# An encoder layer on one core: the first two feed-forward tiles without Strassen, the down GEMM's first sums on VectorE, one norm's sums two tiles later

## The chip, the cores and the metric

The kernel runs on one NeuronCore of a Trainium2 chip. The metric is the device time of one execution in microseconds; lower is better. Three executions of the kernel before took 1586.12, 1586.13 and 1588.37 us, the median is 1586.13 us. The engines are named as the profile names them: PE is the matrix engine (TensorE), DVE is VectorE, ACT is ScalarE, POOL is GpSimd, and SP is the engine whose queue issues nearly all DMAs.

## The reference

One layer of a streaming encoder is computed for 1024 prompt frames and 8 x 16 sample frames, together 1152 rows of 1024 features. Cut to what matters here:

```python
x  = x + rmsnorm(merged @ w_out, g_post1)          # output GEMM, first residual
h2 = rmsnorm(x, g_pre2)
up = h2 @ w_ffn_up                                 # 1024 -> 2 x 2816
a, g = split(up)
act = gelu(causal_conv3(a) + b_dw) * g
x  = x + rmsnorm(act @ w_ffn_down, g_post2)        # 2816 -> 1024
```

Ahead of it lie the three branches (state space, pooling, memory attention) and their gates, which the change does not touch. Everything is float32. The reference's tolerance is met by splitting each operand into a high and a low part of a reduced 32-bit type, so that one product takes three matmuls: high x high, high x low, low x high.

## The kernel before

**Layout.** Activations lie transposed: 128 features on the partitions, rows along the free axis, in three chunks of 384 rows (chunk 0, 1, 2). A weight tile is 128 output features by eight blocks of 128 inputs. One output tile for one chunk is thus 8 x 3 = 24 matmuls of 128x384 (`proj`, which calls `mm3`), collected in one PSUM bank. There are four banks with the tag `c` (in the profile `pc`) and four with the tag `s` (`ps`).

**Splitting.** `split` makes the high part by an ACT copy and the low part by a DVE subtraction, unless it is given another engine. In the profile these are the pairs `whi`/`wlo` (weights), `mhi`/`mlo`, `h2hi`/`h2lo`, `bB`/`bT` (operands of the up GEMM), `dhi`/`dlo` and `dB` (operands of the down GEMM). Both lines of `split` (L63, L64) serve all of them.

**The output GEMM** (`phase_o`) runs over the chunks and in each over eight tiles f of 128 features (`out`). ACT copies each result out of PSUM into `merged` (in the profile `mg`) and squares it; DVE adds the squares into `ssa`. `sums` brings the sums of squares over the partitions by one-column matmuls on PE (L1072) and takes the inverse root on POOL (L86). `row_bcast` spreads that over the partitions: three ACT operations (`diag`, L94) and one PE matmul (L96). `resid` applies the first norm and adds the input x, which it loads two tiles at a time; it writes the sum back to DRAM (`Dx2`) and collects a second sum of squares. `norm` applies the second norm. The sums, the resid and the norm of chunk c-1 are woven between the tiles of chunk c; for chunk 1 the second `sums` stands behind tile f = 4 of chunk 2 (`NF = (0, 5, 4)`), which is where PE asks for it. Chunk 2 itself has no following chunk: its resid and norm are woven into the first work of the up GEMM.

**The up GEMM** treats 22 tiles ff, each of one tile of `a` and one of `g`. For chunks 0 and 1 it uses Strassen's method in Winograd's form over (a, g) x (two halves of the 1024 inputs): seven products of 12 matmuls instead of eight, thus 84 matmuls for both tiles and both chunks instead of 96. This needs four sums of weights per tile (`up_w`: S1 to S4, each then split) and four sums of activations, made once (T1 to T4, split once; B11, B21, B22 and in the change B12 are the quarters themselves). `up_prod` issues one product and evacuates it. Chunk 2 is always done plainly (`up_last`). For ff = 0 and 1 the weight sums are made on DVE, for later ones on POOL. In `phase_u` the two first tiles load and split their weights a second time for chunk 2, since the Strassen operands took the buffers:

```python
for s in self.first:
    self.raws[s.ff] = self.up_raw(s.ff)
    s.aw = self.load_w(None, pool=self.w2, r=self.raws[s.ff][0])
    self.up_last(s, "a"); self.up_act(s); self.up_wg(s); ...
```

**The down GEMM** (`phase_d`) takes 22 blocks of 128 inputs: two whole ones first (`first`, 24 banks of six matmuls), then four groups of four by the same seven-product method, then four whole ones. Products are added up by DVE in SBUF tiles `M` and `y2` (`evac`, L1476 and L1478; the four subtractions of L1608 belong to the first part). A `group` is a generator that loads, sums and splits the operands of one group while PE works on the part ahead of it; its eight sums (L1436 to L1439 for weights, L1444 to L1447 for activations) and four of its splits (S1 to S4) run on POOL.

**What sets the order.** The program is emitted in the order of the Python code, and a scheduler then orders each engine's queue by a simulated timeline. High priority, `issue_after` and `keep_in_program_order` bend this by hand. Each engine then runs its queue strictly in order, and so does SP with its DMAs.

Of the kernel before, what the change touches and what calls it, by code (L numbers as in the profile page):

```python
# [32 lines left out]
class K:  # L33
# [27 lines left out]
    def split(self, hi, lo, src, eng=None):  # L61
        nc = self.nc
        nc.scalar.activation(hi, src, AF.Copy)  # L63
        (eng or nc.vector).tensor_sub(lo, src, hi)  # L64

    def load_raw(self, src, shape=(128, 8, 128)):
# [963 lines left out]
    def phase_o(self):  # L1030
# [6 lines left out]
        if True:  # L1037
# [75 lines left out]
            def norm(c, rs):  # L1113
# [9 lines left out]
                for f in range(8):  # L1123
                    V.scalar_tensor_tensor(oT[:, f, :], oT[:, f, :], self.vec[:, V_GPRE2 + f:V_GPRE2 + f + 1], rb,  # L1124
                                           op0=OP.mult, op1=OP.mult)
                    if c == 2:
                        self.split(self.hhi2[:, f, :], self.hlo2[f], oT[:, f, :])

# [5 lines left out]
            ss = []  # L1134
            NF = (0, 5, 4)
            self.B = {}
            lo, up = slice(0, 4), slice(4, 8)
            h0, h1 = self.merged[0], self.merged[1]
            for c in range(3):
                ss.append(ssa())  # L1140
                for f in range(8):
                    self.pin_sq = c == 2
                    if c == 2 and f == 2:
                        self.raws = {0: self.up_raw(0)}
                    out(c, f)
                    if c:
# [16 lines left out]
            s0 = self.up_begin(0)  # L1163
            self.up_w(s0)

            op("B22", h1[:, up])
            V.tensor_sub(h0[:, lo], h1[:, lo], h0[:, lo])
            V.tensor_sub(h1[:, lo], h1[:, up], h1[:, lo])
            V.tensor_sub(h1[:, up], h1[:, up], h0[:, lo])
            op("T2", h1[:, up])  # L1170
            op("T1", h0[:, lo])
            V.tensor_sub(h0[:, up], h0[:, up], h1[:, lo])
            op("T3", h1[:, lo])
            op("T4", h0[:, up])
            self.raws[1] = self.up_raw(1)
            s1 = self.up_begin(1)

            def prods(s, *ps):
                for p in ps:
                    self.up_prod(s, p)  # L1180
# [12 lines left out]
            norm(2, rs)  # L1193
            prods(s1, 7, 3, 4)
            self.first = s0, s1

# [24 lines left out]
    def up_w(self, s, eng=(None,) * 4):  # L1221

        G = self.nc.vector if s.ff < 2 else self.nc.gpsimd
        ra, rg = self.raws[s.ff]
# [13 lines left out]
        s1, s2 = stage()  # L1238
# [15 lines left out]
    def up_prod(self, s, p):  # L1254
# [95 lines left out]
    def phase_d(self):  # L1350
# [6 lines left out]
        with ExitStack() as ctx:  # L1357
# [42 lines left out]
            def group(g):  # L1400

                s = _S()
                s.g, s.A, s.B = g, {}, {}
                yield s
# [39 lines left out]
                G.tensor_sub(b11, b12, b11)  # L1444
                G.tensor_sub(b12, b22, b12)
                G.tensor_sub(b22, b22, b11)
                G.tensor_sub(b21, b21, b22)  # L1447
# [396 lines left out]
```

## Time and profile before

| | |
|---|---|
| median of three executions | 1586.13 us |
| the profiled execution: time, span | 1587.11 us, 1585.3 us |
| mean granted PE clock | 0.984 |
| PE busy | 97% of the span |
| DVE, ACT, POOL busy | 65%, 37%, 31% |
| DMA | 163.44 MB, mean 103 GB/s |

The profile is that of one execution, whose time is 1.81 us above its span and 0.98 us above the median of the three. PE is busy nearly all the time, so what matters is where it is not, and where its granted clock falls. The slices of the page show two such places inside the kernel: the clock digits fall to 8 in slices 19 and 20 of 40 (each 39.6 us long), which is the passage from the output GEMM to the up GEMM, and DVE is at 8 and 7 tenths around slice 34, where the down GEMM starts. "Busy" of a matmul overlaps the next one's, so a rate is read from starts, not from durations.

### The profile page before, as it was taken

How to read it: one execution, taken by the hardware profiler on the slowest of the kernel's cores; microseconds unless marked ns; L12 is line 12 of the kernel's file. 1: busy time of each engine (PE TensorE's matmuls, PEld its weight loads, DVE VectorE, ACT ScalarE, POOL GpSimd, SP SyncE). 2: the span in 40 equal slices, each digit the busy share in tenths (PEclk: the TensorE clock that was granted, in tenths of full speed). 3: DMA queues.
4: the chain of work that ended last, by engine and by line, in shares of the span. 5: the costliest groups of instructions: out<-in, count | busy, mean ns of one | idle time of the engine just before them, and what ended most of it. 6: DMA issues, size and time to landing. Idle time of an engine off the chain costs nothing.

```text
span 1585.3 us, 22927 instructions
## 1 busy us (share of the span) xinstructions
PE 1539.2 (97%) x8964; PEld 1506.2 (95%) x8964; DVE 1035.0 (65%) x1619; ACT 589.0 (37%) x902; POOL 487.1 (31%) x447
## 2 busy tenths in 40 slices
PE   7999999999999999998989999999999999999996
PEld 7999998888999999998979999999999998999996
DVE  7956986656533463648777655665656569788866
ACT  8313444434312250534444333333333343233321
POOL 0000010000111234200025444444344327665546
PEclk9999999999999999999889999999999999999998
DMA  7533334422422244223123121212121234122315
GB/s 266 168 102 102 107 108 162 151 88 75 158 75 70 81 128 138 98 92 108 47 100 128 56 84 71 83 55 84 70 70 69 80 128 141 60 100 95 92 64 169
DMA packets 98604, 163.44 MB, mean 103 GB/s; under 512 B 23232, under 2 KB 68672, under 8 KB 98496
## 3 DMA queue, kind: packets, MB, share of 16 engines
q1 hardware_dynamic: 98064, 161.75, 31.0%
q8 instruction: 70, 1.15, 0.3%
q14 instruction: 38, 0.31, 0.1%
q10 hardware_dynamic: 432, 0.23, 0.0%
HBM read 119.52 MB, written 42.42 MB: 102 GB/s over the span
## 4 chain that ended last, share of the span: by engine, by line
PE 81%; DVE 9%; DMA 3%; ACT 3%; issue 2%; POOL 1%; SPq 0%; POOLq 0%; DVEq 0%; ACTq 0%
PE pc L107 15%; PE pc L103 15%; PE pc L106 15%; PE ps L103 11%; PE ps L106 11%; PE ps L107 11%; DVE dB L64 1%; DMA Ts<-DG 1%; PE ps L849 1%; DMA DG<-gs 1%; ACT hhi L126 1%; DMA dwr<-in_w_down 1%; PE ps L1072 1%; DVE mg L1124 1%; DVE wlo L64 0%
## 5 line engine op out<-in xcount | busy, mean ns | idle before, releaser
L103 PE MATMUL pc<-hhi,whi 128*128 128x384 f32 x760 | 258.2, 340 | 6.6 <-ACT hhi L126 6.6
L107 PE MATMUL pc<-hhi,wlo 128*128 128x384 f32 x760 | 257.1, 339 | 0.7 <-DVE wlo L64 0.7
L106 PE MATMUL pc<-hlo,whi 128*128 128x384 f32 x760 | 257.5, 339 | 0.1
L63 ACT ACTIVATE whi<-rawt 128x1024 fp32r<-128x1024 f32 (+1 forms) x103 | 107.7, 1046 | 187.0 <-PE pc L106 86.5
L64 DVE TENSOR_TENSOR wlo<-rawt,whi 128x1024 fp32r<-128x1024 f32 (+1 forms) x103 | 127.4, 1239 | 56.3 <-ACT whi L63 55.8
L103 PEld LDWEIGHTS pc<-hhi,whi 128*128 128x128 f32 x760 | 143.8, 189 | 9.1 <-ACT hhi L126 6.6
L107 PEld LDWEIGHTS pc<-hhi,wlo 128*128 128x128 f32 x760 | 143.6, 189 | 3.0 <-DVE wlo L64 1.3
L106 PEld LDWEIGHTS pc<-hlo,whi 128*128 128x128 f32 x760 | 143.7, 189 | 2.8 <-DVE hlo L127 0.7
L200 DVE TENSOR_TENSOR sg<-pc,rb 128x384 f32<-128x384 f32 x95 | 52.3, 554 | 117.3 <-PE pc L107 116.1
L107 PE MATMUL pc<-h2hi,wlo 128*128 128x384 f32 x352 | 119.1, 338 | 2.2 <-DVE wlo L64 2.1
L103 PE MATMUL pc<-h2hi,whi 128*128 128x384 f32 x352 | 118.3, 336 | 0.0
L106 PE MATMUL pc<-h2lo,whi 128*128 128x384 f32 x352 | 118.2, 336 | 0.0
L63 ACT ACTIVATE S<-S 128x512 fp32r<-128x512 f32 x88 | 55.2, 630 | 158.5 <-PE ps L107 89.8
L64 DVE TENSOR_TENSOR S<-S,S 128x512 fp32r<-128x512 f32 x88 | 72.5, 826 | 56.2 <-ACT S L63 54.2
L924 ACT ACTIVATE sg<-sg,vec 128x384 f32<-128x384 f32 x72 | 44.1, 613 | 141.6 <-DVE sg L200 108.3
L103 PE MATMUL ps<-bT,S 128*128 128x384 f32 x240 | 80.2, 334 | 0.0
L106 PE MATMUL ps<-bT,S 128*128 128x384 f32 x240 | 80.2, 334 | 0.0
L107 PE MATMUL ps<-bT,S 128*128 128x384 f32 x240 | 80.2, 334 | 0.0
L1011 POOL TENSOR_TENSOR mg<-mg,sgl 128x384 f32<-128x384 f32 x24 | 29.2, 1216 | 165.2 <-DVE sgl L1009 162.0
L63 ACT ACTIVATE dhi<-dwr 128x1024 fp32r<-128x1024 f32 x38 | 39.8, 1059 | 96.5 <-PE pc L106 61.5
L107 PEld LDWEIGHTS pc<-h2hi,wlo 128*128 128x128 f32 x352 | 66.1, 188 | 2.8 <-DVE wlo L64 2.8
L103 PE MATMUL pc<-mhi,whi 128*128 128x384 f32 x192 | 66.8, 348 | 0.0
(461 smaller groups left out, 4273.2 us busy)
## 6 DMA issues: line engine op xcount, KB each, us to landing
rawt<-in_w_up SPq DMA_DIRECT2D x48, 512.0 KB, 3.4
Dact<-t SPq DMA_DIRECT2D x22, 576.0 KB, 3.6
rawt<-in_w_gate SPq DMA_DIRECT2D x24, 512.0 KB, 3.5
dwr<-in_w_down SPq DMA_DIRECT2D x22, 512.0 KB, 3.4
Dsg<-sg SPq DMA_DIRECT2D x45, 192.0 KB, 1.9
sgl<-Dsg SPq DMA_DIRECT2D x45, 192.0 KB, 2.4
dBr<-Dact SPq DMA_DIRECT2D x8, 768.0 KB, 5.6
xT<-in_xT SPq DMA_DIRECT2D x12, 384.0 KB, 7.8
```

What stands on the lines that cost most here:

```text
L63: nc.scalar.activation(hi, src, AF.Copy)
L64: (eng or nc.vector).tensor_sub(lo, src, hi)
L103: i = nc.tensor.matmul(out, whi, xhi, start=start, stop=False)
L106: nc.tensor.matmul(out, whi, xlo, start=False, stop=False)
L107: nc.tensor.matmul(out, wlo, xhi, start=False, stop=stop)
L126: a = nc.scalar.activation(hi[:, k, :], x[:, k, :], AF.Copy, scale=g)
L200: self.nc.vector.tensor_mul(sg, b, self.rb[:, c, :])
L849: nc.tensor.matmul(o, va[:, m, 2 * hp + e, :], pT[:, m, :], start=m == 0, stop=m == 1)
L924: self.nc.scalar.activation(sg, sg, AF.Sigmoid, bias=self.vec[:, V_BGATE + m:V_BGATE + m + 1])
L1011: nc.gpsimd.tensor_add(m, m, sp)
L1072: m = nc.tensor.matmul(s3[:, t:t + 1], s[:, t * 128:t * 128 + 128], self.ones[:, 0:1], start=(i, t) == (0, 0), stop=(i, t) == (len(ss) - 1 ...
L1124: V.scalar_tensor_tensor(oT[:, f, :], oT[:, f, :], self.vec[:, V_GPRE2 + f:V_GPRE2 + f + 1], rb, op0=OP.mult, op1=OP.mult)
```

## The change

It has five parts:

1. The tiles ff = 0 and 1 of the up GEMM are done plainly for chunks 0 and 1 as well. Their four weight tiles are split once, during the last chunk of the output GEMM, kept, and used again for chunk 2. S1 to S4 of these two tiles are gone, and so is the second load. ACT copies their results out of PSUM (L1186). B12 is split in addition.
2. T1 to T4 are still made, but first needed by ff = 2. T1 is made right behind chunk 1's norm, T2 to T4 behind the norm of chunk 2 (`issue_after(last.ins)`, where `last` is the last high-part split of that norm, which `split` now returns).
3. `NF = (0, 5, 6)`: the second `sums` of chunk 1 stands behind tile f = 6 of chunk 2.
4. The weight sums of ff = 2 move from POOL to DVE. All Strassen products now take their bank from the tag `s`, which for ff of 2 and above they did already.
5. In the down GEMM the eight sums of group 0 and the low parts of its S1 to S4 move from POOL to DVE.

```diff
-            NF = (0, 5, 4)
+            NF = (0, 5, 6)
...
-                    if c == 2 and f == 2:
-                        self.raws = {0: self.up_raw(0)}
+                    if c == 2 and f in (2, 4):
+                        ff = f // 2 - 1
+                        self.raws[ff] = self.up_raw(ff)
+                        fw.append([self.load_w(None, pool=p, r=r) for p, r in
+                                   zip((self.w1, self.w2 if ff else self.w1), self.raws[ff])])
...
+                            else:
+                                op("B12", h1[:, lo])
+                                op("B22", h1[:, up])
+                                V.tensor_sub(h0[:, lo], h1[:, lo], h0[:, lo])
+                                op("T1", h0[:, lo])
...
-            prods(s0, 1, 2)
-            rs = sums(ss[2])
-            prods(s0, 6, 5)
-            with tc.high_priority():
-                ss2 = resid(2, rs)
-            with tc.issue_after(self.diag.ins):
-                self.up_w(s1)
-            prods(s0, 7, 3, 4)
-            prods(s1, 1, 2)
-            rs = sums(ss2)
-            prods(s1, 6, 5)
-            norm(2, rs)
-            prods(s1, 7, 3, 4)
+            def plain(s, which, c):
+                w, dst = (s.aw, s.a) if which == "a" else (s.gw, s.g)
+                x = [self.B[n] for n in (("B11", "B21"), ("B12", "B22"))[c]]
+                b = self.proj(w, c, 8, lambda kt, c: x[kt // 4][0][:, kt % 4, :],
+                              lambda kt, c: x[kt // 4][1][:, kt % 4, :], pin=True)
+                nc.scalar.activation(dst[:, self.ch(c)], b, AF.Copy)
+
+            plain(s0, "a", 0)
+            rs = sums(ss[2])
+            plain(s0, "g", 0)
+            with tc.high_priority():
+                ss2 = resid(2, rs)
+            plain(s1, "a", 0)
+            plain(s1, "g", 0)
+            plain(s0, "a", 1)
+            plain(s0, "g", 1)
+            rs = sums(ss2)
+            plain(s1, "a", 1)
+            with tc.high_priority():
+                last = norm(2, rs)
+            plain(s1, "g", 1)
...
-        G = self.nc.vector if s.ff < 2 else self.nc.gpsimd
+        G = self.nc.vector if s.ff < 3 else self.nc.gpsimd
...
-            self.raws[s.ff] = self.up_raw(s.ff)
-            s.aw = self.load_w(None, pool=self.w2, r=self.raws[s.ff][0])
             self.up_last(s, "a")
             self.up_act(s)
-            self.up_wg(s)
             self.up_last(s, "g")
...
+                E = V if g == 0 else G
...
-                G.tensor_add(a22, a21, a22)
+                E.tensor_add(a22, a21, a22)
...
-                a_op(s, "S4", a12, G)
+                a_op(s, "S4", a12, E)
```

The code's order does not tell what stands next to what in an engine's queue, so three places are shown. Lines below the edited helper are one higher in the changed kernel in `phase_o`, 13 in the up GEMM's functions, and nine or ten in the down GEMM.

First PE, at the third `sums`, that of chunk 2's second norm. `bT` with `S` is a Strassen product of sums, `bB` with `whi`/`wlo` a plain one; `ssa` and `sq` are the sums of squares. Before:

```order
L107 MATMUL pc<-bB_6892,wlo 128x384
L1072 MATMUL ps<-ones,ssa 128x1 x3
L1072 MATMUL ps<-ones,sq 128x1 x6
L103 MATMUL pc<-bT_7298,S_7448 128x384
L106 MATMUL pc<-bT_7298,S_7448 128x384
L107 MATMUL pc<-bT_7298,S_7448 128x384
```

And now:

```order
L108 MATMUL pc<-bB_7273,wlo 128x384
L1073 MATMUL ps<-ones,ssa 128x1 x3
L1073 MATMUL ps<-ones,sq 128x1 x6
L104 MATMUL pc<-bB_7270,whi 128x384
L107 MATMUL pc<-bB_7270,whi 128x384
L108 MATMUL pc<-bB_7270,wlo 128x384
```

Behind the sums PE now has plain products of B12 and B22 (7270 and 7273), which need no sum of weights or activations; ahead of them it has four plain tiles behind the resid's broadcast where it had five Strassen products.

Second DVE, at the resid of chunk 2 (`mg_4095`), whose sums these are. Before:

```order
L1102 SCALAR_TENSOR_TENSOR mg_4095<-mg_4095,vec,ps 128x384 x2
L64 TENSOR_TENSOR S_7457<-S,S_7457 128x512
L1106 TENSOR_TENSOR mg_4095<-mg_4095,x 128x384
L64 TENSOR_TENSOR S_7460<-S,S_7460 128x512
L1106 TENSOR_TENSOR mg_4095<-mg_4095,x 128x384
L1284 TENSOR_TENSOR ax<-v,pc 128x384
L1064 TENSOR_TENSOR ssa<-ssa,sq 128x384
L1102 SCALAR_TENSOR_TENSOR mg_4095<-mg_4095,vec,ps 128x384 x2
L64 TENSOR_TENSOR wlo<-rawt,whi 128x1024
L1106 TENSOR_TENSOR mg_4095<-mg_4095,x 128x384 x2
L1064 TENSOR_TENSOR ssa<-ssa,sq 128x384
L64 TENSOR_TENSOR wlo<-rawt,whi 128x1024
```

And now (`mg_4093` and `mg_4094` are chunks 0 and 1, whose sums for T2 to T4 these are):

```order
L1202 TENSOR_TENSOR mg_4094<-mg_4094 128x1536
L1103 SCALAR_TENSOR_TENSOR mg_4095<-mg_4095,vec,ps 128x384 x2
L1203 TENSOR_TENSOR mg_4094<-mg_4094,mg_4093 128x1536
L1204 TENSOR_TENSOR mg_4093<-mg_4093,mg_4094 128x1536
L1107 TENSOR_TENSOR mg_4095<-mg_4095,x 128x384 x2
L1065 TENSOR_TENSOR ssa<-ssa,sq 128x384
L1103 SCALAR_TENSOR_TENSOR mg_4095<-mg_4095,vec,ps 128x384 x2
L1107 TENSOR_TENSOR mg_4095<-mg_4095,x 128x384 x2
L1065 TENSOR_TENSOR ssa<-ssa,sq 128x384 x2
L1103 SCALAR_TENSOR_TENSOR mg_4095<-mg_4095,vec,ps 128x384 x2
L1107 TENSOR_TENSOR mg_4095<-mg_4095,x 128x384 x2
L1065 TENSOR_TENSOR ssa<-ssa,sq 128x384 x2
```

Between the resid's pairs of rows the splits of S and of the reloaded weights are gone; two sums of T stand inside the first pair.

Third DVE, early in the down GEMM (`M` are the evacuations of the whole blocks, `dBr` the activations of group 0, `t` the last up tile). Before:

```order
L64 TENSOR_TENSOR dB<-dBr,dB 128x768
L1476 COPY M_11838<-ps 128x384
L1476 COPY M_11838<-pc 128x384
L1476 COPY M_11839<-ps 128x384
L1476 COPY M_11839<-pc 128x384
L1313 TENSOR_TENSOR t<-t,g 128x1152
L1476 COPY M_11839<-ps 128x384
L1476 COPY M_11839<-pc 128x384
```

And now:

```order
L64 TENSOR_TENSOR dB<-dBr,dB 128x768
L1486 COPY M_11783<-ps 128x384
L1454 TENSOR_TENSOR dBr<-dBr 128x2x384
L1486 COPY M_11783<-pc 128x384
L1486 COPY M_11784<-ps 128x384
L1486 COPY M_11784<-pc 128x384
L1326 TENSOR_TENSOR t<-t,g 128x1152
L1486 COPY M_11784<-ps 128x384
L1455 TENSOR_TENSOR dBr<-dBr 128x2x384
L1486 COPY M_11784<-pc 128x384
```

The sums of group 0 (L1454, L1455 here, six more below) stand among DVE's evacuations, and POOL's queue has none of them.

More of the change, by code (lines that the diff above doesn't have):

```diff
@@ L62, in split @@
         nc = self.nc
-        nc.scalar.activation(hi, src, AF.Copy)
+        a = nc.scalar.activation(hi, src, AF.Copy)
         (eng or nc.vector).tensor_sub(lo, src, hi)
+        return a
     def load_raw(self, src, shape=(128, 8, 128)):
@@ L1126, in norm @@
                     if c == 2:
-                        self.split(self.hhi2[:, f, :], self.hlo2[f], oT[:, f, :])
+                        a = self.split(self.hhi2[:, f, :], self.hlo2[f], oT[:, f, :])
+                return a if c == 2 else None
             def op(name, src, eng=None):
@@ L1134, in phase_o @@
             ss = []
-            NF = (0, 5, 4)
-            self.B = {}
+            NF = (0, 5, 6)
+            self.B, self.raws, fw = {}, {}, []
             lo, up = slice(0, 4), slice(4, 8)
@@ L1160, in phase_o @@
                                 V.tensor_sub(h0[:, up], h0[:, up], h0[:, lo])
+                            else:
[3 more added lines that the diff above has]
+                                op("T1", h0[:, lo])
             wms.close()
             self.open_u()
-            s0 = self.up_begin(0)
-            self.up_w(s0)
-            op("B22", h1[:, up])
@@ L1167, in phase_o @@
-            V.tensor_sub(h0[:, lo], h1[:, lo], h0[:, lo])
+            first = []
+            for ff in range(2):
+                first.append(self.up_begin(ff))
+                first[ff].aw, first[ff].gw = fw[ff]
+            s0, s1 = self.first = first
+            def plain(s, which, c):
[4 more added lines that the diff above has]
+                nc.scalar.activation(dst[:, self.ch(c)], b, AF.Copy)
@@ L1169, in phase_o @@
             V.tensor_sub(h1[:, up], h1[:, up], h0[:, lo])
-            op("T2", h1[:, up])
-            op("T1", h0[:, lo])
             V.tensor_sub(h0[:, up], h0[:, up], h1[:, lo])
[L1173 to L1180, printed above, removed]
-            prods(s0, 1, 2)
-            rs = sums(ss[2])
-            prods(s0, 6, 5)
@@ L1185, in phase_o @@
-            with tc.high_priority():
-                ss2 = resid(2, rs)
-            with tc.issue_after(self.diag.ins):
-                self.up_w(s1)
-            prods(s0, 7, 3, 4)
-            prods(s1, 1, 2)
-            rs = sums(ss2)
-            prods(s1, 6, 5)
-            norm(2, rs)
-            prods(s1, 7, 3, 4)
-            self.first = s0, s1
+            with tc.issue_after(last.ins):
+                op("T3", h1[:, lo])
+                op("T2", h1[:, up])
+                op("T4", h0[:, up])
@@ L1259, in up_prod @@
                   3: ("S4", "B22"), 4: ("A22", "T4")}[p]
-        b = (self.pc() if s.ff < 2 else self.sm())[:, 0:384]
+        b = self.sm()[:, 0:384]
         (ah, al), (bh, bl) = s.A[an], self.B[bn]
@@ L1435, in group @@
                 yield
-                G.tensor_add(a22, a21, a22)
-                G.tensor_sub(a21, a11, a21)
-                G.tensor_sub(a11, a22, a11)
-                G.tensor_sub(a12, a12, a11)
+                E.tensor_add(a22, a21, a22)
+                E.tensor_sub(a21, a11, a21)
+                E.tensor_sub(a11, a22, a11)
+                E.tensor_sub(a12, a12, a11)
                 b_pair(s, ("B22", "T4"))
                 b_op(s, "B22", b22)
-                a_op(s, "S4", a12, G)
+                a_op(s, "S4", a12, E)
                 yield
[L1444 to L1447, printed above, removed]
+                E.tensor_sub(b11, b12, b11)
+                E.tensor_sub(b12, b22, b12)
+                E.tensor_sub(b22, b22, b11)
+                E.tensor_sub(b21, b21, b22)
                 b_op(s, "T4", b21)
                 yield
-                a_op(s, "S1", a22, G)
+                a_op(s, "S1", a22, E)
                 b_pair(s, ("T1", "T2"))
@@ L1453, in group @@
                 yield
-                a_op(s, "S3", a21, G)
+                a_op(s, "S3", a21, E)
                 b_pair(s, ("T3",))
@@ L1457, in group @@
                 yield
-                a_op(s, "S2", a11, G)
+                a_op(s, "S2", a11, E)
                 b_op(s, "T2", b22)
```

## The prediction, made before the changed kernel ran

> **What bounds the kernel now.** I read the page first, then stretches of time, then PE's waits, then PE's rows around each wait.
>
> ```profile
> span 1585.3 us, 22927 instructions
> PE 1539.2 (97%) x8964; PEld 1506.2 (95%) x8964; DVE 1035.0 (65%) x1619; ACT 589.0 (37%) x902; POOL 487.1 (31%) x447
> ```
>
> PE is the bound over the whole span, so the change must be judged by where PE does not run dense. By stretches (start and end, length, then busy time and count per engine, the granted clock, DMA):
>
> ```profile
> 726.99:841.41 114.42, 99.45 (x515) 96.72 (x515) 91.74 (x126) 55.11 (x93) 22.89 (x22) 0.88 0.29 98
> 775.73:793.20 17.47, 17.47 (x84) 17.20 (x85) 16.30 (x23) 8.07 (x14) 1.71 (x1) 0.83 0.25 76
> 817.60:841.41 23.81, 21.62 (x123) 20.88 (x122) 21.51 (x21) 14.05 (x17) 14.50 (x14) 1.00 0.33 114
> 860.00:1296.00 436.00, 436.00 (x2507) 436.00 (x2506) 254.71 (x264) 166.19 (x229) 180.63 (x184) 1.00 0.23 80
> 1296.69:1335.44 38.75, 35.21 (x194) 34.63 (x193) 38.37 (x43) 13.22 (x15) 22.67 (x9) 0.96 0.21 68
> ```
>
> The fourth row is the up GEMM in its steady state: PE never waits and a matmul takes 436.00/2507 = 0.174 us. I call that dense. The first row is the stretch that the change rewrites. It runs from the first matmul of chunk 2's tile f = 1 to the first product of ff = 2, and PE's clock is 0.88 there. The last row is the start of the down GEMM up to its first plain tile; there DVE is busy 38.37 of 38.75 us. Who made PE wait (total, times, longest):
>
> ```profile
> PE ps L1072 <- DVE ssa L1064: 10.7, 3, 6.4
> PE ps L103 <- DVE M L1608: 3.5, 1, 3.5
> PE pc L107 <- DVE wlo L64: 2.8, 3, 2.1
> PE pc L106 <- DVE bT L64: 1.8, 1, 1.8
> ```
>
> All four lie in the two stretches, but for 0.7 us of the third. PE's own rows (start, duration) show what each costs:
>
> ```profile
> 731.07 0.34 PE L107 MATMUL pc<-mhi,wlo 128*128 128x384 f32 x1
> 731.24 0.81 PE L96 MATMUL ps<-diag,ones 128*128 128x384 f32 x2
> 731.59 0.63 PE L103 MATMUL pc<-mhi,whi 128*128 128x384 f32 x1
> 732.06 0.34 PE L106 MATMUL pc<-mlo,whi 128*128 128x384 f32 x1
> ...
> 744.19 0.34 PE L107 MATMUL pc<-mhi,wlo 128*128 128x384 f32 x1
> 748.47 0.77 PE L1072 MATMUL ps<-ones,ssa 128*128 128x1 f32 x3 [3.94 <-DVE ssa L1064]
> ...
> 772.14 0.72 PE L1072 MATMUL ps<-ones,ssa 128*128 128x1 f32 x6
> 772.72 0.81 PE L1072 MATMUL ps<-ones,sq 128*128 128x1 f32 x6
> 773.45 0.45 PE L103 MATMUL pc<-bT,S 128*128 128x384 f32 x1
> 775.73 0.69 PE L106 MATMUL pc<-bT,S 128*128 128x384 f32 x1 [1.84 <-DVE bT L64]
> ...
> 793.33 0.34 PE L107 MATMUL pc<-bB,wlo 128*128 128x384 f32 x1
> 800.04 0.77 PE L1072 MATMUL ps<-ones,ssa 128*128 128x1 f32 x3 [6.37 <-DVE ssa L1064]
> ```
>
> A broadcast delays PE by 732.06 - 731.07 - 2 x 0.174 = 0.64 us. Twelve passes of a `sums` take 773.45 - 772.14 = 1.31 us, 0.109 each, when nothing waits. The waits come from DVE, which makes S and T and adds squares in one queue. And each wait is paid twice: after 775.73 the clock of the second row above is 0.83, that is (1 - 0.83) x 17.47 = 3.0 us lost at half rate.
>
> **The first stretch before, against dense.** It holds 7 tiles of the output GEMM's chunk 2, the 14 products of ff = 0 and 1 (2 x 84 matmuls, as many as 7 tiles), their four chunk-2 tiles, and that of `a` of ff = 2: 19 x 24 = 456 matmuls x 0.174 = 79.3 us. Added are 48 passes x 0.109 = 5.2 and 4 broadcasts x 0.64 = 2.6: 87.1 us. It takes 114.42, so 27.3 us are waits and half clock.
>
> **Part 1, plain tiles.** They add 2 x 12 = 24 matmuls on PE, all on the path: 24 x 0.174 = +4.2 us, so the stretch dense is 91.3 us. What they remove (S1 to S4 of two tiles, their splits, four 512 KB loads with their splits) lies on DVE, ACT and SP. This is worth nothing by itself, but it takes away what the four waits stood behind. The wait for bT goes, since the first product of sums now comes some 50 us after T's start; that for wlo (2.08 us inside 817.60:841.41) goes, since nothing is loaded again. ACT takes the eight new evacuations, beside PE.
>
> **Part 3, the sums two tiles later.** PE asks for them at 726.99 + 6 x 4.17 + 0.64 = 752.7 instead of 744.4. Before they were ready at 748.5. In DVE's queue ahead of them eight S operations of 128x512 are gone (about 0.6 each, half of the 1.13 below: -4.9), and two or three low parts of 1024 are new (+2.3 to +3.4). On SP two more weight loads now stand ahead of the load of x for rows 6 and 7. I take no wait, with some 5 us to spare.
>
> **Part 2, the next thing that is late: the second sums of chunk 2.** The durations:
>
> ```profile
> L1060 ACT ACTIVATE sq<-mg 128x384 f32<-128x384 f32 x35 | 17.5, 522 | 11.9 <-DVE mg L1106 10.3 <-DVE ssa L1064 1.1
> L1085 ACT ACTIVATE mg<-pc 128x384 f32<-128x384 f32 x16 | 7.8, 486 | 27.1 <-PE pc L107 27.1
> 786.20 1.13 DVE L1102 SCALAR_TENSOR_TENSOR mg<-mg,vec,ps 128x384 f32<-128x384 f32 x2
> 792.73 1.02 DVE L1106 TENSOR_TENSOR mg<-mg,x 128x384 f32<-128x384 f32 x2
> 759.85 4.29 DVE L1124 SCALAR_TENSOR_TENSOR mg<-mg,vec,ps 128x384 f32<-128x384 f32 x8 [7.38 <-PE ps L96]
> 815.87 2.43 DVE L64 TENSOR_TENSOR h2lo<-mg,h2hi 128x384 fp32r<-128x384 f32 x5
> ```
>
> I follow PE from 752.7: sums 1.97 -> 754.6; tile and broadcast 4.81 -> 759.4; plain tile 763.6; sums 1.31 -> 764.9; plain tile 769.1; broadcast of the resid, which I let wait 0.4 for `diag` -> 770.1; four plain tiles -> 774.3, 778.5, 782.6, 786.8. There PE asks again. ACT's queue has the resid's first square behind the evacuation of the tile that ends at 778.5. So: evacuation to 779.1, two squares to 780.1. Then DVE does three pairs of rows, each two scalings (1.13), two additions (1.02) and two sums (about 1.0) with some 0.2 of handing over, 3.3 us: rows 3 to 8 are ready at 782.6, 786.1, 789.3, the last square at 789.9. PE goes on at 790.2 where 786.8 + 1.97 = 788.8 would be dense: **+1.4**.
>
> Is the clock lost there? The nearest row is 772.14 to 775.73: 3.6 us with passes, one matmul and 1.84 of idling, after which 3.0 us were lost. The other end is the wait of 2.08 before 837.5, after which the clock stayed 1.00: nothing lost. The stretch here (786.8 to 790.2, passes only) is like the first, so I take **+2.5**, from 0 to 3.0. The Trainium skill ("TensorE: Matmul & The Clock Gate", Part 1) says that the clock falls after an idle window of about 3.4 us. No whole window is idle here, and by that rule the term would be 0 and the time 2.5 lower; but at 775.73 the trace lost it after less idling.
>
> Behind the last norm (broadcast, then a plain tile of 4.17, DVE eight rows 4.29 and one low part 0.5, about 0.85 after the broadcast's start) PE waits for the first `h2lo`: 0.85 + 4.29 + 0.5 - 0.64 - 4.17 = **+0.9**. Before, 36 matmuls covered it.
>
> T2 to T4, S of ff = 2 and their splits are made under the five chunk-2 tiles (20.9 us) and two products (4.2). On DVE that is h2lo 8 x 0.49, T 3 x 1.7, S 8 x 0.6, two and a half convolution steps of 1.4: some 17 to 20 us, so no wait. S of ff = 2 on DVE costs nothing for that reason.
>
> Sum of the stretch: 91.3 + 0.4 + 1.4 + 2.5 + 0.9 = 96.5 against 114.4: **-17.9 us**.
>
> **Part 5, the down GEMM.** DVE's rows at its start, with POOL's two beside them and three later rows:
>
> ```profile
> 1297.43 1.41 DVE L1308 SCALAR_TENSOR_TENSOR t<-ax,vec,t 128x1152 f32<-128x1152 f32 x1
> 1298.76 0.55 DVE L1476 COPY M<-ps 128x384 f32<-128x384 f32 x1
> 1299.23 0.95 DVE L64 TENSOR_TENSOR dB<-dBr,dB 128x768 fp32r<-128x768 f32 x1
> 1300.10 0.55 DVE L1476 COPY M<-pc 128x384 f32<-128x384 f32 x1
> 1300.56 2.80 DVE L1309 SCALAR_TENSOR_TENSOR t<-ax,vec,t 128x1152 f32<-128x1152 f32 x1
> 1303.29 2.61 DVE L64 TENSOR_TENSOR dB<-dBr,dB 128x768 fp32r<-128x768 f32 x1
> ...
> 1300.31 1.84 POOL L1444 TENSOR_TENSOR dBr<-dBr 128x768 f32<-128x768 f32 x1 [4.96 <-PE ps L107]
> 1302.23 2.85 POOL L1445 TENSOR_TENSOR dBr<-dBr 128x768 f32<-128x768 f32 x1
> ...
> 1310.80 1.74 DVE L64 TENSOR_TENSOR dc<-cr,dc 128x1536 fp32r<-128x1536 f32 x1
> 1323.61 1.21 DVE L64 TENSOR_TENSOR dlo<-dwr,dhi 128x1024 fp32r<-128x1024 f32 x1
> ```
>
> While POOL runs a sum, a DVE operation of two tiles takes 2.80 instead of 1.41, and 2.61 instead of 0.95. So the POOL sums cost DVE about as much as they would on DVE. From start to start DVE's prices are: copy 0.47, 128x768 0.87, convolution 1.33, 128x1024 about 1.13, `dc` 1.67. PE's 24 whole banks of six matmuls last 1296.69 + 24 x 1.04 = 1321.7 if none waits; the 25th needs the 17th evacuation. Ahead of that DVE now has three steps of t (4.0), four dB and four sums of 768 (7.0), dc (1.7), three dlo and one sum of 1024 (4.5), 17 evacuations (8.0): 1297.4 + 25.2 = 1322.6. PE waits 0.9 there, and by the same count 0.4 eight banks later; at 3.5 with a half clock behind it before. The first plain tile starts at 1296.69 + 32 x 1.04 + 1.3 = 1331.3 instead of 1335.44: **-4.1 us**. The ends: -5.4 (dense) and 0, were DVE as late as before.
>
> **Sum.** -17.9 - 4.1 = -22.0. The profiled execution would span 1563.3 us. Its time (1587.11) lies 0.98 us above the median of the three, 1586.13, so the forecast for the median is 1586.13 - 22.0 = **1564 us**.
>
> **Rivals.**
> - *The moved sums are still late.* Two 512 KB loads and two Dx2 writes stand before the last x on SP; ACT's squares stand behind splits that wait for these loads. For it: x came last before, and DVE idled for it. Against: 5 us to spare. If they came as much after 752.7 as they did after 744.4 before (4 us, and 2.5 for the clock): 1564 + 6.5 = 1570.5.
> - *DVE stays the bound of the down GEMM.* It takes over some 13 us of work. If the stretched rows come from something other than POOL, DVE is late by what it was plus part of that, and the 4.1 us are lost, or turn into +3: 1568 to 1571.
> - *No clock loss at 790, and shorter waits:* 1564 - 2.5 - 1 = 1560.5.
> - *Slower.* T2 and T4 take the buffers of `merged` 2 and 1, and S those of the first tiles' weights. Were all of S and T made only after the last chunk-2 tile has freed its buffers, some 18 to 20 us of DVE work would follow, of which two products cover 4.2; with half clock behind it PE would lose about 19, giving 1583. It decides from 22 us on, so it needs the POOL-like stretching of DVE as well: 1587 to 1590. Against: T2's buffer is free once h2lo is made, some 20 us earlier.
> - *The plain tiles buy nothing*, the waits being replaced by equal ones at the new sums: 1586 + 4.2 - 4.1, within 0.2% (3.2 us, about what a measurement of this kernel can tell from no change). Against: DVE's queue there has lost its other work.
>
> **Chances.** The forecast, 1560.5 to 1568, has 0.60; late sums 0.12, late down GEMM 0.12, shorter waits 0.10, no gain 0.03, slower 0.03. The range 1559 to 1571.5 holds the first four but their tails, about 0.8. Faster by over 0.2%: 0.94; within: 0.03; slower: 0.03.
>
> **What would show it.** Right: the stretch from chunk 2's second tile to the first product of ff = 2 takes 95 to 98 us; PE's longest wait there is for the square or sum of chunk 2's resid, 2 to 3 us; no wait for bT or wlo; the clock falls once, behind that wait. In the down GEMM no wait for L1618 (L1608 before), a wait of about 1 us for an evacuation, and L1322 and dB of normal length. Wrong: a wait of 3 us or more at the sums behind f = 6, at the first S or T product, or at a bank in the down GEMM.

## The result

The changed kernel takes 1572.69 us, the median of four runs (1568.66 to 1575.39), against 1587.25 (1586.12 to 1588.37) for the kernel before. The ratio is 0.991 (95%: 0.988 to 0.993), 14.6 us faster. The forecast was 1564, with a range up to 1571.5: the direction came true, about a third of the gain did not.

The page of the profiled execution (time 1571.99):

```profile
span 1570.2 us, 22880 instructions
PE 1535.1 (98%) x8988; PEld 1503.1 (96%) x8988; DVE 1018.3 (65%) x1606; ACT 583.3 (37%) x895; POOL 447.9 (29%) x427
```

The span is 15.1 us shorter. Stretches of time, with the columns of before (length, busy time and count of PE, PEld, DVE, ACT and POOL, granted clock, DMA): the stretch that the change rewrites, two pieces of it, the down GEMM's start up to its first plain tile, and a piece near the end:

```profile
725.38:828.88 103.50, 96.05 (x539) 93.63 (x539) 70.39 (x100) 48.14 (x86) 21.08 (x15) 0.95 0.27 90
773.43:776.90 3.47, 3.47 (x12) 3.17 (x11) 2.65 (x3) 0.00 (x0) 0.00 (x0) 0.51 0.00 0
797.50:801.00 3.50, 3.50 (x13) 3.50 (x13) 0.00 (x0) 0.99 (x3) 0.28 (x1) 0.54 0.02 6
1284.16:1318.63 34.47, 33.63 (x194) 33.09 (x193) 34.20 (x48) 13.00 (x15) 0.00 (x0) 1.00 0.22 71
1500.84:1503.72 2.88, 2.88 (x11) 2.88 (x11) 2.88 (x7) 0.52 (x1) 0.00 (x0) 0.50 0.00 0
```

The first stretch takes 103.50 us where it took 114.42: -10.9, and -17.9 was forecast. The down GEMM's start takes 34.47 instead of 38.75: -4.3, and -4.1 was forecast. The rest balances: the first stretch begins 1.6 us earlier, and 1.7 are lost behind the down GEMM's start, nearly all of it at the last row, where the clock is halved behind a wait of 1.98 us that was 1.69 before. So the 7 us that are missing lie in the first stretch. Who makes PE wait, in the whole run:

```profile
PE ps L97 <- ACT diag L95: 5.0, 2, 4.8
...
PE ps L1073 <- DVE ssa L1065: 1.3, 2, 0.9
PE ps L1073 <- ACT sq L1061: 1.2, 1, 1.2
...
PE ps L104 <- DVE y L1486: 0.8, 1, 0.8
...
PE pc L107 <- DVE h2lo L64: 0.5, 1, 0.5
```

The waits for bT, for wlo in this stretch and for L1608 (now L1618) are gone, as they should be. The first line is new: 4.8 us for `diag`, where the forecast had let the broadcast of chunk 2's resid wait 0.4. PE's rows there (start, duration):

```profile
767.44 0.34 PE L108 MATMUL pc<-bB,wlo 128*128 128x384 f32 x1
772.56 1.65 PE L97 MATMUL ps<-diag,ones 128*128 128x384 f32 x2 [4.79 <-ACT diag L95]
773.43 1.09 PE L104 MATMUL pc<-bB,whi 128*128 128x384 f32 x1
```

PE stands still from 767.8 to 772.6. Then it runs at half clock: the broadcast takes 1.65 instead of 0.81, and up to 776.90 the clock is 0.51. Who was late is read backwards, in the rows of ACT, POOL and DVE:

```profile
764.07 0.16 ACT L85 ACTIVATE rs_v<-ps 128x3 f32<-128x3 f32 x1
...
771.52 0.98 ACT L95 ACTIVATE diag<-ident,rs_y 128x128 f32<-128x128 f32 x3 [5.89 <-POOL rs_y L87]
...
753.51 0.85 POOL L87 TENSOR_TENSOR rs_y<-rs_v,mhalf 128x3 f32<-128x3 f32 x1 [25.43 <-ACT rs_v L85]
...
764.37 7.11 POOL L87 TENSOR_TENSOR rs_y<-rs_v,mhalf 128x3 f32<-128x3 f32 x1 [6.89 <-ACT rs_v L85]
796.94 0.85 POOL L87 TENSOR_TENSOR rs_y<-rs_v,mhalf 128x3 f32<-128x3 f32 x1 [25.45 <-ACT rs_v L85]
...
762.35 1.75 DVE L1170 TENSOR_TENSOR mg<-mg,mg 128x1536 f32<-128x1536 f32 x1
764.02 3.42 DVE L64 TENSOR_TENSOR bB<-mg,bB 128x1536 fp32r<-128x1536 f32 x2
767.36 1.75 DVE L64 TENSOR_TENSOR bT<-mg,bT 128x1536 fp32r<-128x1536 f32 x1
769.02 1.76 DVE L1202 TENSOR_TENSOR mg<-mg 128x1536 f32<-128x1536 f32 x1
```

ACT gave `rs_v` in time, at 764.2, and idled 5.9 us for POOL. POOL's power of 128x3, the inverse root, takes 0.85 us at the sums ahead of these and behind them (753.51, 796.94), and 7.11 here. DVE meanwhile runs five operations without a gap, each with both inputs in SBUF: T1's subtraction, the low parts of B12, B22 and T1, and the first of the subtractions for T2 to T4 (L1202), which the scheduler moved up. They end at 770.78, and the power 0.70 later. That is a theory so far. The Trainium skill ("SBUF — State Buffer", Who interferes with whom) states the rule: a DVE instruction with two SBUF inputs contends with a GpSimd instruction that reads SBUF. The same page of the Trainium skill (Summary: rules for kernel authors) has the second one to issue blocked "until the first finishes". The rows agree in kind. But by that POOL would have waited for the low part that was running, until 765.77, and not for three more operations.

### The profile page after: what moved, and what is told of

The parts are those of the page before. It is cut to its first block, busy times and chain, and to the rows that moved or that the text cites. A ratio compares the mean times of both kernels' runs of the same rounds, so it can differ in the third digit from the quotient of the medians.

```text
span 1570.2 us, 22880 instructions
## 1 busy us (share of the span) xinstructions
PE 1535.1 (98%) x8988; PEld 1503.1 (96%) x8988; DVE 1018.3 (65%) x1606; ACT 583.3 (37%) x895; POOL 447.9 (29%) x427
## 4 chain that ended last, share of the span: by engine, by line
PE 85%; DVE 7%; DMA 3%; issue 2%; ACT 1%; POOL 1%; SPq 0%; POOLq 0%; ACTq 0%; DVEq 0%
PE pc L108 16%; PE pc L107 16%; PE pc L104 16%; PE ps L104 11%; PE ps L107 11%; PE ps L108 11%; DMA Ts<-DG 1%; DMA DG<-gs 1%; PE ps L850 1%; POOL rs_y L87 1%; DVE mg L1125 0%; PE ps L97 0%; PE ps L764 0%; PE ps L816 0%; DVE Xs L599 0%
## 5 line engine op out<-in xcount | busy, mean ns | idle before, releaser
L63 ACT ACTIVATE whi<-rawt 128x1024 fp32r<-128x1024 f32 (+1 forms) x99 | 103.5, 1047 | 189.0 <-PE pc L107 85.5
L64 DVE TENSOR_TENSOR wlo<-rawt,whi 128x1024 fp32r<-128x1024 f32 (+1 forms) x99 | 122.4, 1238 | 56.3 <-ACT whi L63 56.0
L63 ACT ACTIVATE S<-S 128x512 fp32r<-128x512 f32 x80 | 50.3, 629 | 149.2 <-PE ps L108 88.9
L64 DVE TENSOR_TENSOR S<-S,S 128x512 fp32r<-128x512 f32 x80 | 66.6, 835 | 49.7 <-ACT S L63 47.7
L87 POOL TENSOR_TENSOR rs_y<-rs_v,mhalf 128x3 f32<-128x3 f32 (+1 forms) x13 | 18.8, 1445 | 174.8 <-ACT rs_v L85 174.7
L107 PEld LDWEIGHTS pc<-h2lo,whi 128*128 128x128 f32 x352 | 66.0, 187 | 0.8 <-DVE h2lo L64 0.8
```

The lines of the kernel that those rows point to most:

```text
L63: a = nc.scalar.activation(hi, src, AF.Copy)
L87: nc.gpsimd.tensor_tensor(y, v, self.mhalf[:, 0:n], op=OP.pow)
L107: nc.tensor.matmul(out, whi, xlo, start=False, stop=False)
```

## The experiments

**The wait, taken apart.** Theory A: the power is late because of DVE's run. Theory B: it is slow by itself, or because of transfers. The first kernel measures the power alone:

```
for kind, n in ((None, 0), (wide, 6), (narrow, 20), (bank, 20), (mix, 5)):
    first = V.tensor_add(gate, x); v = scalar.activation(first)
    y = gpsimd.tensor_tensor(v, mhalf, pow)
    n times: kind on V          # wide: 128x1536, both inputs in SBUF
```

> None of the reference is computed here (the outputs are zeros): POOL's 128x3 power is measured by itself, 20 times, each started just after DVE has begun a run of one kind: nothing (4 times); six subtractions of 128x1536 with both inputs in SBUF; twenty additions of 128x384 with both inputs in SBUF; twenty scalings of 128x384 with one input in PSUM; five pairs of a 128x1536 subtraction and a copy out of PSUM. Theory A (POOL can't read SBUF while DVE runs operations with two SBUF inputs one behind another): 0.85 us alone and beside the scalings; 1 to 10 us beside the six subtractions and the twenty additions, ending behind a boundary of two DVE operations or behind the last; at most 2.5 us beside the pairs. Theory B (the 7.11 us came from POOL itself or from transfers): about 0.85 us in all five.

Its rows of POOL, one for each kind but the last (2.00 us there too), and DVE's run of `wide`:

```profile
17.68 0.85 POOL L1751 TENSOR_TENSOR rs_y<-rs_v,mhalf 128x3 f32<-128x3 f32 x1 [1.21 <-ACT rs_v L1749]
19.74 2.00 POOL L1751 TENSOR_TENSOR rs_y<-rs_v,mhalf 128x3 f32<-128x3 f32 x1 [1.21 <-ACT rs_v L1749]
...
67.43 1.26 POOL L1751 TENSOR_TENSOR rs_y<-rs_v,mhalf 128x3 f32<-128x3 f32 x1 [9.93 <-ACT rs_v L1749]
...
112.57 0.85 POOL L1751 TENSOR_TENSOR rs_y<-rs_v,mhalf 128x3 f32<-128x3 f32 x1 [10.02 <-ACT rs_v L1749]
...
19.28 10.10 DVE L1722 TENSOR_TENSOR wide<-x 128x1536 fp32r<-128x1536 f32 x6
```

Alone, and beside operations with one input in PSUM (the fourth row), it takes 0.85 us. Beside operations with two SBUF inputs it takes 2.00 (wide) and 1.26 (narrow), 0.7 behind the end of the operation that was running. Theory B falls. But no boundary is passed over here, so 7.11 us is not reached.

Two edits of the changed kernel shorten the run beside the power. The first makes T1 and the three subtractions later, the second moves the splits of B12 and B22 too:

```
-    op("B12", h1[:, lo]); op("B22", h1[:, up])      # second kernel only
-    V.tensor_sub(h0[:, lo], ...); op("T1", h0[:, lo])
...
     ss2 = resid(2, rs)
+    with tc.issue_after(self.diag.ins), tc.issue_after(self.row1.ins):
+        (the lines taken out above, then the three subtractions for T2 to T4)
```

> The changed kernel with T1 (its subtraction and its low part) and the three subtractions for T2 to T4 made behind the second row of chunk 2's resid, so that DVE's run beside the power ends 3.4 us earlier, with the low part of B22. Theory A: the power ends about 0.7 us behind that, near 768.1 where it was 771.48: 3.7 us long instead of 7.11, and PE's wait for diag 1.4 us instead of 4.8. Three DVE operations (5.0 us) then stand in the resid's window instead, so the second sums of chunk 2 wait up to 5 us longer: the time is within 2 us of the changed kernel's 1572.7. Theory B: the power stays near 7 us and the wait at 4.8.

> As the kernel before it, with the splits of B12 and B22 behind chunk 2's resid rows too: no DVE operation with two SBUF inputs is left beside the power. Theory A: the power takes 0.85 us, PE waits at most 0.4 us for diag, and the clock isn't lost behind it; the second sums wait 4 to 6 us since all the splits now stand among the resid's rows: about 1569. Theory B: the power stays near 7 us and the time is above the changed kernel's 1572.7.

The power and DVE's last operations beside it, in the first:

```profile
768.67 2.29 POOL L87 TENSOR_TENSOR rs_y<-rs_v,mhalf 128x3 f32<-128x3 f32 x1 [6.89 <-ACT rs_v L85]
...
766.65 3.61 DVE L64 TENSOR_TENSOR bB<-mg,bB 128x1536 fp32r<-128x1536 f32 x2
```

and in the second, with no such operation left:

```profile
767.23 0.85 POOL L87 TENSOR_TENSOR rs_y<-rs_v,mhalf 128x3 f32<-128x3 f32 x1 [6.37 <-ACT rs_v L85]
```

Again 0.70 behind the run's end (770.26), and 0.85 without a run; PE's wait for `diag` is gone in both. In the first, 3.7 us and a wait of 1.4 were expected. T1's subtraction had stood at the front of the run, so that the run ends 4.8 us earlier against the power's start and not 3.4; the power starts within the run's last operation and passes no boundary. The times are 1568.19 (ratio 0.988, 0.986 to 0.990) and 1573.16 (0.991, 0.990 to 0.993). The second gave back all of it: with the splits among the resid's rows, PE waits 5.8 us for the second sums of chunk 2. That wait was expected, but the time is 4 us longer than expected, and 2.0 us of clock that were not counted are lost behind the wait (0.50 over 2.13 us, then 0.76 over 4.00).

```profile
PE ps L1073 <- DVE ssa L1065: 6.2, 2, 5.8
```

The reverse edit makes the run one operation longer, and tells whether the power's end follows the run's end:

```
     op("T1", h0[:, lo])
+    t1 = self.B["T1"]; V.tensor_sub(t1[1], h0[:, lo], t1[0])     # the same values again
```

> The changed kernel with one more DVE operation in the run: T1's low part is written a second time, with the same values, behind the subtraction that ended the run (+1.67 us). Theory A (in this place POOL is shut out until the run of operations with two SBUF inputs ends): the power ends 0.70 behind the longer run, 8.8 us long instead of 7.11, PE waits 6.4 to 6.5 us for diag instead of 4.8, and the first stretch is 105 us, 1.7 longer. Rival A' (it gets in after a fixed time, or at the fourth boundary): 7.1 us and a wait of 4.8, as before.

```profile
765.48 8.78 POOL L87 TENSOR_TENSOR rs_y<-rs_v,mhalf 128x3 f32<-128x3 f32 x1 [6.89 <-ACT rs_v L85]
...
771.80 1.75 DVE L1173 TENSOR_TENSOR bT<-mg,bT 128x1536 fp32r<-128x1536 f32 x1
```

8.78 us, and PE's wait is 6.45: as theory A had it. The time is 1579.53 (0.994, 0.992 to 0.996). The stretch of 109.5 us is longer than the expected 105, since the second sums also wait 2.3 us instead of 0.9, and more clock is lost.

Last, an operation of another kind in the run. The first plain tile's evacuation goes from ACT to DVE, as a copy out of PSUM, in one kernel between the low parts of B12 and B22, in the other two operations later, behind T1's:

```
-    nc.scalar.activation(dst[:, self.ch(0)], b, AF.Copy)
+    with tc.issue_after(low.ins):          # B12's low part; in the second kernel T1's
+        V.tensor_copy(dst[:, self.ch(0)], b)
```

In the code T1's subtraction also goes ahead of the splits, and in the first kernel the splits of B22 and T1 go behind the copy. In the first kernel's trace the other operations of DVE and ACT beside the power stand in the order of the changed kernel.

> The changed kernel with the first plain tile's evacuation on DVE instead of ACT, in the middle of the run of low parts: a 128x384 copy out of PSUM, 0.55 us, between the low parts of B12 and B22. The run as a whole is 0.5 us longer. Theory A (POOL gets in where DVE runs an operation without two SBUF inputs): the power ends within 1 us of that copy's start if it has started by then, 2 to 2.5 us long, PE waits at most 0.5 us for diag and the time falls 5 to 6.5 us, to 1566 to 1568. Rival (only DVE's idle time lets it in): the power ends 0.7 behind the run, 7.6 us long, PE waits 5.3, and the time is that of the changed kernel or 0.5 more.

> The control to the kernel with the copy out of PSUM in the run: the same evacuation on DVE instead of ACT, so that ACT's and POOL's queues are as there, but two operations later, behind T1's low part. Theory A (the place of the copy lets POOL in): the power ends 0.70 behind T1's low part, 5.0 to 5.7 us long, PE waits 3.2 us for diag, and the clock falls behind it: the first stretch 100 to 102 us, the time 1568 to 1571. Rival B' (the evacuation's leaving ACT's queue is what helped): the power takes 2.3 us, no wait for diag, 96.5 us and 1564, as with the copy two operations earlier.

The first (POOL, DVE, and the first stretch):

```profile
764.01 2.32 POOL L87 TENSOR_TENSOR rs_y<-rs_v,mhalf 128x3 f32<-128x3 f32 x1 [6.67 <-ACT rs_v L85]
...
763.87 1.76 DVE L64 TENSOR_TENSOR bB<-mg,bB 128x1536 fp32r<-128x1536 f32 x1
765.54 0.55 DVE L1187 COPY ax<-pc 128x384 f32<-128x384 f32 x1
766.00 1.75 DVE L64 TENSOR_TENSOR bB<-mg,bB 128x1536 fp32r<-128x1536 f32 x1
...
725.25:821.70 96.45, 93.79 (x538) 91.93 (x538) 70.82 (x101) 48.09 (x85) 16.30 (x15) 0.98 0.29 96
```

The second:

```profile
766.10 5.66 POOL L87 TENSOR_TENSOR rs_y<-rs_v,mhalf 128x3 f32<-128x3 f32 x1 [6.70 <-ACT rs_v L85]
...
770.97 0.56 DVE L1189 COPY ax<-pc 128x384 f32<-128x384 f32 x1
```

Where the copy stands decides. Early, the power ends 0.70 behind the operation before the copy, the wait for `diag` is gone, and the kernel takes 1564.41 us (0.986, 0.984 to 0.988), less than the expected 1566 to 1568. Late, with the same instructions on ACT, PE waits 3.1, and it takes 1571.80 (0.989, 0.988 to 0.991), 0.8 above the expected range. So it isn't that ACT had one thing less to do.

**What lets POOL in.** Two more kernels measured the power beside runs of six and five operations: with other kinds and eight starting points, and then with ACT's high parts, a MEMSET ahead on POOL and matmuls on TensorE beside it.

```
for kind in (wide, low, place, real):  8 starts each          # the first
for kind in range(4):  6 starts each; matmuls if kind >= 2; memset if kind % 2   # the second
```

> None of the reference is computed here (the outputs are zeros): POOL's 128x3 power beside runs of six DVE operations again, now in four kinds (subtractions of 128x1536 into another tile; low parts of 128x1536 as in the kernel; subtractions in place of 128x1536; the kernel's own run: one subtraction in place, three low parts, one subtraction in place), each eight times, with the power started 0 to 1.5 us later within the run from one to the next. In the measurement before, it always ended 0.78 behind the first boundary of two operations; in the changed kernel it passed three boundaries and ended 0.70 behind the run. Theory A1 (a boundary lets it in or not by the kind of operation): passed over in the runs with low parts or subtractions in place, whatever the start; ended at the first boundary in the first kind. Theory A2 (it hangs on when in an operation it starts): passed over at some of the eight starts, in all kinds alike. Theory A3 (something else of the kernel is needed): never more than 2.6 us.

> None of the reference is computed here (the outputs are zeros): the power beside the kernel's own run of five DVE operations, now with what stood around it in the kernel: ACT makes the high parts that the low parts wait for (all 24); a MEMSET on POOL just ahead (every second group of six); 60 matmuls on TensorE at the same time (the last two groups). Alone, the power had always ended behind the first boundary of two operations or the next (2.4 us at most). Theory A1 (low parts that have waited for ACT leave no boundary to POOL): passed over in all four groups, up to 7 us. Theory A2 (POOL's other work or TensorE's reads matter): passed over only in the groups that have them. Theory A3 (none of these): 0.85 to 2.4 us in all.

It took 0.87 to 2.38 us in the first and 0.85 to 2.43 in the second: A3 in both. In isolation POOL gets in at the next boundary, in the changed kernel it does not. The changed kernel, profiled once more:

> The changed kernel once more, for a second profile beside its times. The power of chunk 2's resid took 7.11 us and ended 0.70 behind the end of a run of four DVE operations. Theory A1 (it is shut out for as long as the run has no gap): again near 7.1 us, PE's wait for diag 4.8, the first stretch 103 to 104 us. Theory A2 (it gets in at one of the ends of the four, by chance): 2.0, 3.7, 5.4 or 7.1 us, the wait 0 to 4.8, and the stretch 97 to 104 us. Median 1569 to 1575 either way.

7.11 us and a wait of 4.79 again (1573.97 us; 0.992, 0.990 to 0.993). The kernels below with part 4 or part 5 undone show 7.11 and 4.8 again, so in this place it is no chance. The power's end follows the run's end in runs of three lengths, with two, three and four boundaries passed (5.66, 7.11 and 8.78 us).

What closes the boundaries stays open. It is not the kernel as such: in the kernel before, the power of the same resid starts within the second of three low parts, which ends at 777.35, and ends 0.71 behind it, while the third runs without a gap.

```profile
773.93 5.08 DVE L64 TENSOR_TENSOR bT<-mg,bT 128x1536 fp32r<-128x1536 f32 x3
...
776.35 1.71 POOL L86 TENSOR_TENSOR rs_y<-rs_v,mhalf 128x3 f32<-128x3 f32 x1 [8.18 <-ACT rs_v L84]
```

**The other parts, undone one at a time.** The sums at f = 4 again (part 3), the down GEMM's sums on POOL again (part 5), the sums of S for ff = 2 on POOL again (part 4):

```
-    NF = (0, 5, 6)
+    NF = (0, 5, 4)
...
-    E = V if g == 0 else G
+    E = G
...
-    G = self.nc.vector if s.ff < 3 else self.nc.gpsimd
+    G = self.nc.vector if s.ff < 2 else self.nc.gpsimd
```

> Undoes the third part alone: the second sums of chunk 1 asked for at f = 4 again, 744 by PE's count of before. By the trace of the changed kernel their last square is done 747.4 there. Theory (the move was needed): PE waits 2.5 to 4 us for the square or sum at f = 4 and loses 0 to 2 us of clock behind it; but the first norm is then 4 to 5 us earlier, so that the run of DVE splits ends before the power starts, which saves up to 6.5: the net is -4 to +3 on 1572.7. Rival (the move bought nothing in itself): no wait at f = 4, and the time falls to about 1566.

> Undoes the fifth part alone: the sums of the down GEMM's first group on POOL again. By the sum of the prediction: +4.1 us (ends 0 and +5.4), with PE's wait of 3.5 us for the adding evacuation back, a stretch from the first product to the first plain tile of 38 to 39 us instead of 34.5, and DVE's 128x768 and 128x1152 operations stretched to 2.6 to 2.8 us beside POOL's sums. Rival: the gain came from the down GEMM's other timing, and nothing changes (within 1 us).

> Undoes the fourth part alone: the sums of S for ff = 2 on POOL again. The prediction costs this part at nothing: no wait for S or T at ff = 2 in either, within 2 us of 1572.7. Rival: POOL's 128x512 sums are held up by DVE's run of low parts there, S comes late and PE waits for it in the products of ff = 2: +1 to +5 us.

Part 3 undone (PE's waits in the first stretch):

```profile
PE ps L1073 <- DVE ssa L1065: 7.1, 3, 5.4
```

PE waits 5.4 us at f = 4, more than expected, but none for `diag`: the power takes 2.08 us, since the run is over earlier. The stretch is 102.9 us, the time 1573.11 (0.992, 0.990 to 0.993). The wait that the two tiles saved is about as long as the one that they brought to `diag` (5.4 and 4.8).

Part 5 undone (the down GEMM's start, and two of its rows on DVE):

```profile
1287.57:1326.33 38.76, 35.21 (x194) 34.63 (x194) 38.47 (x43) 13.13 (x15) 22.68 (x9) 0.96 0.20 68
...
1291.43 2.80 DVE L1322 SCALAR_TENSOR_TENSOR t<-ax,vec,t 128x1152 f32<-128x1152 f32 x1
1294.16 2.61 DVE L64 TENSOR_TENSOR dB<-dBr,dB 128x768 fp32r<-128x768 f32 x1
```

38.76 us, as before the change, with the stretched rows and the wait of 3.5 for L1618 back. The time, 1576.79 (0.993, 0.991 to 0.995), lies 2.8 us above the changed kernel's 1573.97 on the same chip, though single runs of the two overlap.

Part 4 undone brings one wait among the products of ff = 2, for an evacuation:

```profile
PE ps L104 <- DVE u L1287: 1.2, 1, 1.2
```

A low part of weights just ahead of that evacuation (842.10) takes 2.32 us beside POOL's sums where another took 1.22 in the changed kernel (835.27). The time does not show it: 1572.48 (0.991, 0.989 to 0.992).

**A faster version.** The second sums of chunk 1 go to f = 5, so that DVE's run is over when the power starts, and the subtractions for T2 to T4 go behind the resid's second row:

```
-    NF = (0, 5, 6)
+    NF = (0, 5, 5)
...
     ss2 = resid(2, rs)
+    with tc.issue_after(self.row1.ins):
+        (the three subtractions for T2 to T4)
```

> The changed kernel with the second sums of chunk 1 one tile earlier (f = 5, their last square was done 3.7 us before PE asked at f = 6), and the three subtractions for T2 to T4 behind the second row of chunk 2's resid. DVE's run of splits then ends at about 764.5, when the power starts. Theory A: the power takes 1 to 2 us, PE waits at most 0.5 us for diag without losing clock, the sums at f = 5 wait 0 to 1 us, the second sums of chunk 2 wait 1 to 3 us: 1563 to 1566. Theory B: the power stays near 7 us: 1571 to 1574.

```profile
PE ps L1073 <- DVE ssa L1065: 2.1, 2, 1.7
```

The power ends 0.70 behind the run (2.27 us), and PE does not wait for `diag`. But it waits 1.7 us for the sums at f = 5, more than expected, and loses clock behind it; 1567.84 (0.988, 0.987 to 0.990), above the expected 1563 to 1566. ACT had a weight's split, which waited for its load, ahead of chunk 1's last squares, and DVE had its low part ahead of the last addition:

```profile
746.09 1.06 ACT L63 ACTIVATE whi<-rawt 128x1024 fp32r<-128x1024 f32 x1 [2.41 <-DMA rawt<-in_w_up]
747.05 1.33 ACT L1061 ACTIVATE sq<-mg 128x384 f32<-128x384 f32 x3
```

The next kernel puts that split behind them:

```
+    late = self.sq, self.sqadd               # chunk 1's last square and addition
...
+    with tc.issue_after(late[0].ins), tc.issue_after(late[1].ins):
         fw[-1].append(self.load_w(None, pool=..., r=self.raws[ff][1]))   # ff = 1
```

> The kernel with the second sums of chunk 1 at f = 5 and the late subtractions, and with the split of the plain weights of ff = 1 for g put behind chunk 1's last square on ACT and DVE (there it stood ahead of the squares and waited for its load). Theory: the wait of 1.7 us for the sums at f = 5 and the clock lost behind it (1.5) go; the power ends as before, with no wait for diag: the first stretch 93 to 94 us instead of 96.4, the time 3 us below that kernel, 1563 to 1566. Rival: the weights are then late for the tile of g at ff = 1, or the resid's squares take the place of the wait: no change, 1567 to 1568.

```profile
727.05:819.93 92.88, 91.93 (x539) 90.47 (x539) 70.21 (x100) 48.16 (x86) 16.27 (x15) 1.00 0.29 101
```

92.88 us at a clock of 1.00, 3.5 less than in the kernel ahead of it (96.42), and 1563.03 us (0.985, 0.984 to 0.986): faster than the kernel before and than the changed one. Against the kernel ahead of it the medians are 4.8 us apart, but the two profiled executions only 0.2 (1563.20 and 1563.03), since in the later one the stretch begins 1.4 us later and 1.9 us more are lost behind it.

## Why the prediction was right and wrong

PE's rows at the two later sums of the changed kernel and at the first `h2lo`, and one of DVE with the last addition of chunk 1's squares:

```profile
751.10 0.72 PE L1073 MATMUL ps<-ones,ssa 128*128 128x1 f32 x6
...
791.80 0.34 PE L108 MATMUL pc<-bB,wlo 128*128 128x384 f32 x1
793.04 0.80 PE L1073 MATMUL ps<-ones,ssa 128*128 128x1 f32 x6 [0.91 <-DVE ssa L1065]
795.09 1.50 PE L1073 MATMUL ps<-ones,sq 128*128 128x1 f32 x12 [1.24 <-ACT sq L1061]
796.45 0.42 PE L104 MATMUL pc<-bB,whi 128*128 128x384 f32 x1
...
807.96 0.44 PE L107 MATMUL pc<-h2lo,whi 128*128 128x384 f32 x1 [0.52 <-DVE h2lo L64]
...
747.73 1.02 DVE L1065 TENSOR_TENSOR ssa<-ssa,sq 128x384 f32<-128x384 f32 x2
```

- **The step that failed** is the term of 0.4 us for the resid's broadcast waiting for `diag`. It measured 4.8 us of waiting, 0.5 in the broadcast at half clock (0.87 from its start to the next matmul's instead of 0.35) and 1.7 in the matmuls behind it ((1 - 0.51) x 3.47), 7.0 in all. With the copy in the run the stretch is 96.45 us where 96.5 was forecast: this one term is the stretch's whole miss (103.50 - 96.45 = 7.05 us). That the time of that kernel, 1564.4, meets 1564 too is in part luck: its four runs lie between 1562.75 and 1566.32. The prediction counted what POOL's sums do to DVE, in the down GEMM, and not what DVE's run does to a POOL instruction on the path; no rival named it. The kernel before gave a sign: the power at 776.35, shown above, took 1.71 us instead of 0.85 beside DVE's run.
- **The dense stretch** of 91.3 us was right: with three short waits of 0.4 to 0.5 us left the last kernel needs 92.9.
- **The second sums of chunk 2**: 1.4 was forecast. PE's last matmul ahead of them starts at 791.80, the next at 796.45 (rows above); less 0.17 and 1.97 for the passes that is 2.5. **The clock behind it**: 2.5 was forecast, and 1.6 was lost (3.50 us at 0.54). Together 4.1 instead of 3.9: two errors that cancel. The clock fell twice in this stretch, not once.
- **The first `h2lo`**: 0.9 forecast, and PE's matmuls stand 0.86 apart there instead of 0.17: 0.7.
- **Part 3** had no wait, as forecast, but 2.7 us to spare instead of 5: the last addition of chunk 1 (the first of the two in the last row) ended at 748.3, PE asked at 751.1. With the sums at f = 4 and at f = 5 PE starts 0.15 behind the end of that same addition; the expectations for these two kernels took the last square, at 747.4, which is one reason why both waits came out longer. Undoing it showed a side that the prediction did not cost: moving the norm two tiles later moved DVE's splits onto the power.
- **Parts 1 and 4**: no wait for bT, S or T, and none for wlo in this stretch, as forecast. Part 4, costed at nothing, kept away a wait of 1.2 us, which is too small for the times to tell.
- **Part 5**: -4.3 for -4.1, with a wait of 0.8 us for an evacuation where 0.9 was forecast, and undoing it brings the stretch's 4.3 us back, of which 2.8 show in the medians.

## What to carry to other kernels

A short instruction on the path costs what the other engines let it cost: before a dense run is put beside it, ask whether both read SBUF, and who holds up whom, in both directions. When a step is moved later, follow all that hangs on it, and not only the wait that it is to save. The place of one 0.55 us copy was worth 7 us here (1571.80 and 1564.41), because in one of two places it broke the run in time.

## What the runs showed of the hardware

- A POOL operation of 128x3 that reads SBUF ends 0.70 us behind the DVE operation with two SBUF inputs that holds it up. Alone that is the one that runs when it starts (at most 2.43 us over 76 powers), and so it was in the kernel before (1.71). In the changed kernel it is the last of the gapless run (7.11, 8.78 and 5.66 us for runs of three lengths). Which of the two it will be no run here tells ahead. A DVE operation whose one input lies in PSUM lets it in (2.32).
- TensorE's clock was halved for some 3 us behind a wait of 4.79 us, behind one of 1.98 (the stretch from 1500.84), and behind two of 0.91 and 1.24 with passes of one column between them. It was not behind one of 2.08 in the kernel before (at 837.46), nor behind 0.43. The length of the wait alone does not decide: at the place of the 1.98, near the end, the clock stayed 1.00 behind waits of 1.69 (the kernel before), of 1.61 (part 5 undone) and of 1.52 and 0.95 one soon after the other (part 4 undone), and fell behind shorter ones, of 0.98 and 0.95 (the longer run, 0.65 over 3.50 us) and of 0.19 and 1.60 (the last kernel, 0.57 over 2.72). The Trainium skill ("TensorE: Matmul & The Clock Gate", Part 1) names an idle window of about 3.4 us; only the first of these waits is that long, so here the measurement decides. Part of the scatter of the times, up to 7.5 us between runs of one kernel, may come from such waits; that is argued, not shown.
